# Slots, residual rows and final operations of the last products, and half of the divisions moved from ScalarE to VectorE

## The chip, the cores and the metric

The kernel runs on one core of a Trainium2 chip. The metric is the device time of one execution in microseconds, as the median of several runs. A profile of one execution gives the spans, waits and transfers that are read below. Its engines are TensorE (PE, and PEld for its weight loads), VectorE (DVE), ScalarE (ACT), GpSimd (POOL) and SyncE (SP, which issues most DMAs).

## The reference, cut to what matters

One layer of an encoder, for 1024 prompt rows and 32 sample rows with a cache of 512. All values are float32.

```python
def mla_attend(q_nope, q_rope, qpos, k_nope, k_rope, v, kpos):      # branch A, 8 heads, 64-wide values
    s = (einsum(q_nope, k_nope) + einsum(q_rope, k_rope)) * MLA_SCALE
    mask = (kpos // CHUNK) <= (qpos // CHUNK)                        # CHUNK = 64
    p = softmax(where(mask, s, NEG))
    return einsum('bhqs,bshd->bqhd', p, v)
...
merged = sigmoid(g_a) * (o_a @ w_proj_a) + sigmoid(g_b) * (o_b @ w_proj_b)   # branch B: stick-breaking attention
x = x + gt1 * rms_norm(merged @ w_out, g_post_mix)
h2 = rms_norm(x, g_pre_ffn) * (1 + sc2) + sh2
u = h2 @ w_up                                                        # 1024 -> 2 * 2816
y = causal depthwise conv of width 3 over u;  a, b = split(y)
f = (gelu(a) * b) @ w_down                                           # 2816 -> 1024
x = x + gt2 * rms_norm(f, g_post_ffn)
```

## The kernel before

A float32 product is made as three products of rounded parts: `hi` (line 61, ScalarE) writes the high half of a tile, `lo` (line 64, VectorE) the rest, and TensorE adds up high by high, high by low and low by high. The stages follow each other: modulation and projections, the stick-breaking attention, latents, the latent attention (about 675 to 945 us of the profile), merge, up-projection with convolution, down-projection (the end, from about 1560 us).

**The order on each engine** is not the program's. The framework plans it when the kernel is built: it plays the program through with costs of its own, gives each engine its next ready instruction, those earlier in the program first, and puts in the waits. The order on an engine and on a DMA queue is then fixed. Tiles come from pools; a tag has a set number of buffers, and a new tile waits until the oldest one of its tag is released.

**The latent attention** works head by head on pairs of query tiles of 128 rows (`attend`): tile `i` has `(i + 1) * 128` keys. For each tile, scores go to one or two PSUM banks, and `mla_weights` (from line 493 on) takes the maximum on VectorE (line 499), the exponential with its sum on ScalarE (line 507), the reciprocal `ri` of the sum on VectorE (line 514), and multiplies the whole tile by `ri` on ScalarE (line 515). Then the tiles are transposed (line 542), split (`PTh`, `PTl`) and multiplied by the values (line 555). Products of the other branch (`proj_b`) are planned in between. The second tile of each pair has 256, 512, 768 or 1024 keys.

**The down-projection** (`stage_down`) takes the gated rows `gdn` from DRAM and makes the product in a seven-product scheme on quarters (512 features by 512 rows), each in six steps over the 22 blocks of 128. Its matmuls are lines 1636 to 1638. `product(banks, s, weights, ...)` does one of the seven: at each step it takes weights that `put` has split into one of seven slots, loads the gates (`wr`, two buffers, line 1629), splits them (`wh`, `wl`, two buffers each) and issues 4 x 3 matmuls for each block of 128. `raw` loads weights into three `dr` buffers, and every fourth time into `wr` (a tile of its own, named `d` in the profile). Without a number, `put` takes the slots 0 to 6 in turn. Slots 0 to 3 are called `B` in the profile, 4 and 5 `d`, slot 6 `wh` and `wl`.

The last three products are that of `t3` with index 1 into the banks `X`, that of index 6 into the banks `Z`, whose loop also puts the six `t2` tiles into slots for later (`last`), and the last one, which is written out by hand: for each of four row tiles `t`, gates in blocks of 8 and 3 (line 1741), and 33 matmuls into `X[t]`. Between the first two, `c22[t]` is completed on VectorE (line 1714) and squared on ScalarE (line 1690).

`out` finishes a row tile of 128 rows: it loads the residual row `x1d` (line 1724), squares the half that has just come (`ps`), adds the sum of the other half (`s0`, line 1727, GpSimd), takes the root with `rstd` (lines 92 and 93, GpSimd), multiplies both halves by root and gain `G` (line 1732, VectorE), adds the residual (line 1733) and stores (line 1734). Its `x` and `y` come from tag `u` with five buffers, one of which holds `G`.

Of the kernel before, what the change touches and what calls it, by code (L numbers as in the profile page):

```python
# [8 lines left out]
F32 = mybir.dt.float32  # L9
# [8 lines left out]
P = 128  # L18
# [22 lines left out]
class K:  # L41
# [451 lines left out]
    def mla_weights(self, pieces, w):  # L493
        nc = self.nc
        B = self.tl(self.At, [P, TP], F32, "A")
        np_ = len(pieces)
        mx = self.tl(self.sm, [P, 2], F32, "mx")
        for i, (ps, c0, n) in enumerate(pieces):
            nc.vector.tensor_reduce(mx[:, i : i + 1], ps[:, :n], AX.X, ALU.max, negate=True)
        m = mx[:, 0:1]  # L500
        if np_ == 2:
            mn = self.tl(self.sm, [P, 1], F32, "mn")
            nc.vector.tensor_tensor(mn, mx[:, 0:1], mx[:, 1:2], ALU.min)
            m = mn
        sm = self.tl(self.sm, [P, 2], F32, "sum")
        for i, (ps, c0, n) in enumerate(pieces):
            self.exp = nc.scalar.activation(B[:, c0 : c0 + n], ps[:, :n], AF.Exp, bias=m, accum_out=sm[:, i : i + 1])
        s = sm[:, 0:1]
        rc = self.tl(self.sm, [P, 1], F32, "rc")
        if np_ == 2:  # L510
            nc.vector.tensor_tensor(rc, sm[:, 0:1], sm[:, 1:2], ALU.add)
            s = rc
        ri = self.tl(self.sm, [P, 1], F32, "ri")
        nc.vector.reciprocal(ri, s)
        nc.scalar.activation(B[:, :w], B[:, :w], AF.Identity, scale=ri)
        return B

    def attend(self, h, score, weights, V, out, order=(0, 1, 2, 3)):
# [1063 lines left out]
    def stage_down(self):  # L1582
# [29 lines left out]
        def raw(j, n, e, h):  # L1612
            self.n_raw += 1
            x = self.dn() if self.n_raw < 3 or self.n_raw % 4 else wr
            return load(x.rearrange("p (k c) -> p k c", k=2), j, n, e, h)

        def put(x, i=None):
            n = x.shape[1]
            if i is None:
                i = self.n_slot % len(slots)  # L1620
                self.n_slot += 1
            h, l = (y[:, :n] for y in slots[i])
            self.hi(h, x)
            self.lo(l, x, h)
            return h, l
# [14 lines left out]
        def product(banks, s, weights, first, more=None, part=range(6)):  # L1640
            for i, (j, n) in enumerate(steps):
                if i not in part:
                    continue
                wh, wl = weights(i, j, n)
                gh, gl = gates(s, j, n)
                if more:
                    more(i, j, n)
                for k in range(n):
                    for t in range(4):
                        tk = slice(t * P, t * P + P)  # L1650
                        add3(banks[t], gh[:, k, tk], gl[:, k, tk], wh[:, k], wl[:, k], first and j + k == 0, j + k == NJ - 1)
# [37 lines left out]
        def square(t, x, c):  # L1689
            nc.scalar.activation(junk, x, AF.Square, accum_out=c)  # L1690
# [22 lines left out]
        for t in range(4):  # L1713
            add(c22[t], X[t], c22[t], ALU.add)
            square(t, c22[t], ss[:, 4 + t : 5 + t])

        last = []
        product(Z, 6, lambda i, j, n: put(raw(j, n, 1, 1), (0, 1, 2, 3, 0, 1)[i]), False,
                lambda i, j, n: last.append(put(t2[i], (4, 5, 6, 2, 3, 0)[i])))

        def out(t, done, ps, s0, c0):

            x = tok()
            nc.sync.dma_start(x, self.x1d[t])
            s = self.tl(self.sm, [P, 1], F32, "ss")
            square(t, ps, s)
            nc.gpsimd.tensor_tensor(s, s, s0, ALU.add)  # L1727
            r = self.rstd(s, D, P)
            y = tok()
            for c, f in ((c0, ps), (512 - c0, done)):  # L1730
                c = slice(c, c + 512)
                nc.vector.scalar_tensor_tensor(y[:, c], f, r, G[:, c], ALU.mult, ALU.mult)  # L1732
                nc.vector.tensor_tensor(y[:, c], y[:, c], x[:, c], ALU.add)  # L1733
                nc.sync.dma_start(a["y_p"][0, t * P : t * P + P, c], y[:, c])

        for t in range(4):
            add(c12[t], Z[t], c12[t], ALU.add)
        for t in range(4):
            for k0, n in ((0, 8), (8, 3)):
                x = self.tl(self.W, [P, 1024], F32, "wr")  # L1740
                nc.sync.dma_start(x[:, : n * P].rearrange("p (k c) -> p k c", k=n),
                                  self.gdn[k0 : k0 + n, :, 1536 + t * P : 1536 + t * P + P].rearrange("k p c -> p k c"))
                gh, gl = (y.rearrange("p (k c) -> p k c", c=P) for y in self.wsplit(x, n * P))
                for k in range(n):
                    wh, wl = (y[:, (k0 + k) % 2] for y in last[(k0 + k) // 2])
                    add3(X[t], gh[:, k], gl[:, k], wh, wl, False, k0 + k == NJ - 1)
            out(t, c11[t], c12[t], ss[:, t : t + 1], 512)
            out(4 + t, c22[t], X[t], ss[:, 4 + t : 5 + t], 0)
        G2.release()
        self.F.release()  # L1750
        self.Rp.release()
# [89 lines left out]
```

## Time and profile before

| | |
|---|---|
| median of three runs | 1797.5 us (1796.99 to 1802.86) |
| the profiled execution | 1796.74 us, its span 1794.7 us |
| TensorE, VectorE, ScalarE, GpSimd busy | 97%, 70%, 56%, 14% of the span |
| granted clock of TensorE | 0.994 in the mean |
| HBM traffic | 174.32 MB read, 51.25 MB written |

A row in the order of time has its start, its length, engine, line, operation, what is written `<-` what is read, shapes, and in brackets the idle time of the engine before it with what ended it. A row of a group has count, then busy time in us and the mean of one in ns, then idle time before. A row of waits has the total, the number and the longest.

### The profile page before, as it was taken

What the parts mean: (1) busy time and instruction counts of PE and PEld (TensorE: products, weight loads), DVE (VectorE), ACT (ScalarE), POOL (GpSimd) and SP (SyncE); (2) the same over time, 40 slices, a digit from 0 to 9 for tenths busy, and PEclk for the clock granted to TensorE, in tenths of its full rate; (3) what the DMA queues carried; (4) which work ended last, traced back from release to release, by engine and by line L of the source; (5) the groups of instructions that cost most, each with busy time, mean ns of one, the idle gap of its engine ahead of it and who ended that gap; (6) DMA issues with size and microseconds to landing.
All of it is one profiled execution on the core that took longest, in us unless ns stands there. A gap on an engine that the chain in (4) does not pass through costs nothing. (4 is left out here: it accounts for less than half of the span.)

```text
span 1794.7 us, 30062 instructions
## 1 busy us (share of the span) xinstructions
PE 1733.5 (97%) x11610; PEld 1547.7 (86%) x11610; DVE 1258.4 (70%) x2087; ACT 1005.4 (56%) x1926; POOL 253.3 (14%) x518
## 2 busy tenths in 40 slices
PE   6999999999999999999999999999999999999997
PEld 3988888988888998888888868999999999977876
DVE  4677377576487467777676768977777787788446
ACT  4565366564464469688687357644444454544332
POOL 2112111110111001101000022321111111110001
PEclk9999999999999999999999999999999999999999
DMA  8333332332333112313336542333333323597426
GB/s 316 109 101 106 101 100 74 90 111 83 101 103 85 57 54 77 90 51 95 101 115 218 169 154 83 124 124 124 101 124 126 132 90 124 196 344 260 147 87 224
DMA packets 181710, 227.52 MB, mean 127 GB/s; under 512 B 13349, under 2 KB 129776, under 8 KB 181568
## 3 DMA queue, kind: packets, MB, share of 16 engines
q1 hardware_dynamic: 166048, 182.10, 31.7%
q0 software_dynamic: 15296, 43.42, 6.8%
q8 instruction: 91, 1.49, 0.3%
q14 instruction: 51, 0.42, 0.1%
q10 hardware_dynamic: 224, 0.09, 0.0%
HBM read 174.32 MB, written 51.25 MB: 126 GB/s over the span
## 5 line engine op out<-in xcount | busy, mean ns | idle before, releaser
L61 ACT ACTIVATE wh<-wr 128x1024 fp32r<-128x1024 f32 (+6 forms) x185 | 149.5, 818 | 254.9 <-PE s L1305 83.4
L64 DVE TENSOR_TENSOR wl<-wr,wh 128x1024 fp32r<-128x1024 f32 (+6 forms) x185 | 168.3, 916 | 137.0 <-ACT wh L61 135.5
L68 PE MATMUL mm<-hh,wh 128*128 128x352 f32 x696 | 229.6, 330 | 2.4 <-DVE nat L648 2.4
L69 PE MATMUL mm<-hl,wh 128*128 128x352 f32 x696 | 228.6, 328 | 0.4 <-DVE hl L277 0.4
L70 PE MATMUL mm<-hh,wl 128*128 128x352 f32 x696 | 228.0, 328 | 0.0
L68 PEld LDWEIGHTS mm<-hh,wh 128*128 128x128 f32 x696 | 131.3, 189 | 10.3 <-issue 4.1
L69 PEld LDWEIGHTS mm<-hl,wh 128*128 128x128 f32 x696 | 131.5, 189 | 2.7 <-DVE hl L277 0.9
L70 PEld LDWEIGHTS mm<-hh,wl 128*128 128x128 f32 x696 | 131.6, 189 | 1.2 <-issue 0.4
L542 PE MATMUL tr<-c,A 128*128 128x128 f32 x576 | 93.7, 277 | 4.9 <-ACT A L490 3.6
L1306 PE MATMUL s<-T,wl 128*128 128x256 f32 (+1 forms) x328 | 93.4, 285 | 0.0
L1305 PE MATMUL s<-T,wh 128*128 128x256 f32 (+1 forms) x328 | 93.3, 285 | 0.0
L1304 PE MATMUL s<-T,wh 128*128 128x256 f32 (+1 forms) x328 | 93.3, 284 | 0.0
L486 DVE TENSOR_TENSOR_SCAN A<-A 128x128 f32<-128x128 f32 (+8 forms) x66 | 87.8, 1343 | 0.4
L1442 DVE SCALAR_TENSOR_TENSOR u<-u,c,u 128x1058 f32<-128x1058 f32 x68 | 87.0, 1316 | 1.4 <-ACT u L1439 0.2
L490 ACT ACTIVATE A<-A 128x128 f32<-128x128 f32 (+8 forms) x66 | 44.6, 682 | 74.8 <-DVE A L489 74.3
L64 DVE TENSOR_TENSOR PTl<-tr,PTh 128x512 fp32r<-128x512 f32 x96 | 62.9, 683 | 29.9 <-ACT PTh L61 29.5
L542 PEld LDWEIGHTS tr<-c,A 128*128 128x128 f32 x576 | 67.5, 141 | 14.4 <-ACT A L490 8.1
L1304 PE MATMUL tr<-T,wh 128*128 128x272 f32 (+1 forms) x272 | 77.7, 286 | 0.0
L1306 PE MATMUL tr<-T,wl 128*128 128x272 f32 (+1 forms) x272 | 77.4, 285 | 0.0
L1305 PE MATMUL tr<-T,wh 128*128 128x272 f32 (+1 forms) x272 | 77.3, 284 | 0.0
L64 DVE TENSOR_TENSOR wl<-S,wh 128x1024 fp32r<-128x1024 f32 x40 | 48.9, 1223 | 37.8 <-ACT wh L61 37.8
L1304 PE MATMUL mm<-T,wh 128*128 128x256 f32 (+1 forms) x256 | 73.1, 286 | 0.0
(650 smaller groups left out, 5557.1 us busy)
## 6 DMA issues: line engine op xcount, KB each, us to landing
wr<-in_w_ada_dram SPq DMA_DIRECT2D x48, 512.0 KB, 4.7
wr<-in_w_up_dram SPq DMA_DIRECT2D x44, 512.0 KB, 3.8
dr<-in_w_down_dram SPq DMA_DIRECT2D x43, 512.0 KB, 5.8
wr<-gdn SPq DMA_DIRECT2D x34, 512.0 KB, 3.9
wr<-in_w_in_dram SPq DMA_DIRECT2D x33, 512.0 KB, 4.2
gdn<-u POOLq DMA_DIRECT2D x23, 512.0 KB, 4.8
gd<-nat POOLq DMA_DIRECT2D x48, 176.0 KB, 2.1
t<-gd SPq DMA_DIRECT2D x16, 528.0 KB, 5.2
```

Source lines behind the costliest of these rows:

```text
L61: self.nc.scalar.activation(out, in_, AF.Identity, scale=scale)
L64: return self.nc.vector.tensor_tensor(out, full, hi.bitcast(F32), ALU.subtract)
L68: m(ps, lh, rh, start=start, stop=False)
L69: m(ps, lh, rl, start=False, stop=False)
L70: m(ps, ll, rh, start=False, stop=stop)
L486: nc.vector.tensor_tensor_scan(r, r, r, 0.0, ALU.add, ALU.bypass)
L490: nc.scalar.activation(A[:, :w], A[:, :w], AF.Exp)
L542: nc.tensor.transpose(tr[:, (2 * s + q) * P : (2 * s + q + 1) * P], at[q][:, b * P : b * P + P], self.idt)
L1304: m(ps[:, :n], w[0][:, k], x[0][:, k, c], start=first and k == 0, stop=False, skip_group_check=True)
L1305: m(ps[:, :n], w[0][:, k], x[1][:, k, c], start=False, stop=False, skip_group_check=True)
L1306: m(ps[:, :n], w[1][:, k], x[0][:, k, c], start=False, stop=k == 3, skip_group_check=True)
L1442: nc.vector.scalar_tensor_tensor(y, u[:, w : w + YW], self.cvT[:, w, cc : cc + 1], y, ALU.mult, ALU.add)
```

## The change

The diff, whole but for blank lines:

```diff
@@ mla_weights
         nc.vector.reciprocal(ri, s)
-        nc.scalar.activation(B[:, :w], B[:, :w], AF.Identity, scale=ri)
+        if w % 256 == 0:
+            nc.vector.tensor_scalar(B[:, :w], B[:, :w], ri, None, ALU.mult)
+        else:
+            nc.scalar.activation(B[:, :w], B[:, :w], AF.Identity, scale=ri)
         return B
@@ stage_down
         for t in range(4):
             add(c22[t], X[t], c22[t], ALU.add)
             square(t, c22[t], ss[:, 4 + t : 5 + t])
+        nc.gpsimd.tensor_scalar(ss[:, :8], ss[:, :8], 1.0 / D, EPS, ALU.mult, ALU.add)
         last = []
-        product(Z, 6, lambda i, j, n: put(raw(j, n, 1, 1), (0, 1, 2, 3, 0, 1)[i]), False,
-                lambda i, j, n: last.append(put(t2[i], (4, 5, 6, 2, 3, 0)[i])))
-
-        def out(t, done, ps, s0, c0):
-
-            x = tok()
+        product(Z, 6, lambda i, j, n: put(raw(j, n, 1, 1), (2, 4, 6, 1, 2, 4)[i]), False,
+                lambda i, j, n: last.append(put(t2[i], (3, 5, 0, 6, 1, 2)[i])))
+
+        x1 = [x.rearrange("p k c -> p (k c)") for x in (*t3[:5], *t2[:3])]
+        for t, x in zip((0, 4, 1, 5, 2, 6, 3, 7), x1):
             nc.sync.dma_start(x, self.x1d[t])
-            s = self.tl(self.sm, [P, 1], F32, "ss")
+
+        def out(t, done, ps, c0):
+
+            x = x1.pop(0)
+            s, v, r = (self.tl(self.sm, [P, 1], F32, n) for n in ("ss", "rv", "rs"))
+            y = tok()
+            cd, cp = slice(512 - c0, 1024 - c0), slice(c0, c0 + 512)
+            nc.gpsimd.tensor_tensor(y[:, cd], done, G[:, cd], ALU.mult)
             square(t, ps, s)
-            nc.gpsimd.tensor_tensor(s, s, s0, ALU.add)
-            r = self.rstd(s, D, P)
-            y = tok()
-            for c, f in ((c0, ps), (512 - c0, done)):
-                c = slice(c, c + 512)
-                nc.vector.scalar_tensor_tensor(y[:, c], f, r, G[:, c], ALU.mult, ALU.mult)
-                nc.vector.tensor_tensor(y[:, c], y[:, c], x[:, c], ALU.add)
+            add(y[:, cp], ps, G[:, cp], ALU.mult)
+            nc.gpsimd.tensor_scalar(v, s, 1.0 / D, ss[:, t : t + 1], ALU.mult, ALU.add)
+            nc.gpsimd.tensor_tensor(r, v, self.mhalf, ALU.pow)
+            for c in (cp, cd):
+                nc.vector.scalar_tensor_tensor(y[:, c], y[:, c], r, x[:, c], ALU.mult, ALU.add)
                 nc.sync.dma_start(a["y_p"][0, t * P : t * P + P, c], y[:, c])
@@ the last product, written out
             for k0, n in ((0, 8), (8, 3)):
-                x = self.tl(self.W, [P, 1024], F32, "wr")
+                x = self.dn() if k0 == 0 else self.tl(self.W, [P, 1024], F32, "wr")
                 nc.sync.dma_start(x[:, : n * P].rearrange("p (k c) -> p k c", k=n),
...
-            out(t, c11[t], c12[t], ss[:, t : t + 1], 512)
-            out(4 + t, c22[t], X[t], ss[:, 4 + t : 5 + t], 0)
+            out(t, c11[t], c12[t], 512)
+            out(4 + t, c22[t], X[t], 0)
```

In words: the 32 second tiles of the pairs in the latent attention are multiplied by `ri` on VectorE instead of ScalarE. The last full product takes its weights and the `t2` tiles into other slots. The eight residual rows are loaded into tiles `t3` and `t2` that have been read, all asked for in the program ahead of the last product, and no longer into `u` buffers one by one. The sums of squares are scaled once for all eight, `out` multiplies the earlier half by `G` on GpSimd and the later one on VectorE, and then one operation on VectorE for each half multiplies by the root and adds the residual. The larger gate loads of the last product use the three `dr` buffers (`dn()`).

## Prediction

> **What bounds the kernel now.** I read the page first, then the windows over the places that the change touches, then the order of time there, and last the waits of TensorE.
>
> ```profile
> span 1794.7 us, 30062 instructions
> ...
> PE 1733.5 (97%) x11610; PEld 1547.7 (86%) x11610; DVE 1258.4 (70%) x2087; ACT 1005.4 (56%) x1926; POOL 253.3 (14%) x518
> ```
>
> TensorE is busy for 97% of the span. So work that the other engines gain or lose counts only where TensorE stands still, or behind its last matmul. The windows show where that is. Their columns are length, then busy time and instructions of TensorE, its weight loads, VectorE, ScalarE and GpSimd, then the granted clock, the share of the DMA engines, and GB/s.
>
> ```profile
> 675.00:945.00 270.00, 261.73 (x1761) 229.09 (x1760) 194.42 (x486) 220.06 (x521) 32.04 (x59) 0.99 0.29 88
> ...
> 1700.00:1716.00 16.00, 16.00 (x71) 12.86 (x70) 6.64 (x6) 4.80 (x7) 0.00 (x0) 1.00 0.27 82
> 1719.89:1721.70 1.81, 0.00 (x1) 0.00 (x1) 1.75 (x3) 1.81 (x5) 0.00 (x0) 1.00 0.84 269
> 1722.90:1726.40 3.50, 3.50 (x10) 2.68 (x10) 1.20 (x2) 0.17 (x2) 0.00 (x0) 0.51 0.50 140
> 1769.20:1769.79 0.59, 0.01 (x2) 0.01 (x1) 0.59 (x2) 0.50 (x3) 0.08 (x1) 1.00 0.80 316
> 1769.79:1777.70 7.91, 7.91 (x33) 6.11 (x33) 5.09 (x9) 2.03 (x4) 2.09 (x6) 1.00 0.92 318
> 1777.70:1779.44 1.74, 0.04 (x2) 0.00 (x1) 1.68 (x2) 1.10 (x4) 1.27 (x1) 1.00 0.64 234
> ```
>
> The first row is the latent attention: TensorE lacks 8.3 of 270 us there, ScalarE has 220 us of work (82%), VectorE 194 (72%). The rest is the end of the kernel. TensorE stands for 1.81 us between the product of `t3` and the product of `Z`, and 1.2 us after it has started again its clock is granted at 0.51 for 3.50 us, which costs 3.50 x 0.49 = 1.7 us. In the last product it stands for 0.58 and 1.70 us. Then comes the tail behind the last matmul.
>
> **Part 1, the slots of the last full product.** The seven slots are handed out in turn, and 30 puts come before the product of `Z` with index 6. The last six, of the product of `t3`, fill 3, 4, 5, 6, 0, 1, and slot 2 is free from its beginning. Before, the weights of the first two steps go to slots 0 and 1, which are the last two to come free.
>
> ```profile
> 1715.96 1.06 ACT L61 ACTIVATE wh<-wr 128x1024 fp32r<-128x1024 f32 x1 [4.02 <-PE tr L1637]
> 1716.89 0.69 DVE L1714 TENSOR_TENSOR d<-mm,d 128x512 f32<-128x512 f32 x1 [3.69 <-PE mm L1638]
> 1716.93 1.04 ACT L61 ACTIVATE B<-dr 128x1024 fp32r<-128x1024 f32 x1
> 1717.50 1.22 DVE L64 TENSOR_TENSOR wl<-wr,wh 128x1024 fp32r<-128x1024 f32 x1
> ...
> 1720.43 1.22 DVE L64 TENSOR_TENSOR B<-dr,B 128x1024 fp32r<-128x1024 f32 x1
> ...
> 1721.70 0.50 PE L1637 MATMUL s<-B,wh 128*128 128x512 f32 x1 [1.81 <-DVE B L64]
> ```
>
> The high half of slot 0 (`B<-dr`) is made at 1716.93, as soon as step 4 of `t3` has released it, and its low half comes behind the four additions to `c22` on VectorE, at 1720.43 to 1721.65. TensorE has done its four matmuls that need only high halves by 1719.89 and waits for it. After the change these weights go to slot 2, those of step 1 to slot 4 and those of step 2 to slot 6, the first `t2` tiles to 3, 5 and 0. All but the last of these are free while `t3` still runs; ScalarE has 4.80 and VectorE 6.64 us of work in the 16 us before, so both halves are made there. What is late next is the split of the gates, `wl<-wr,wh`, which ends at 1718.72, over a microsecond before TensorE stops at 1719.89. The stall of 1.81 us goes. The slow stretch goes with it, since no other stall lies in the 3.4 us ahead of it: 3.5 us together. Bounds: nothing is gained if another low half is put in the same place; were `wl` planned behind all four additions (0.6 us from start to start), it would end at about 1720.5, and some 1.1 us of the stall would stay. I take 3.5, because the row has `wl` behind one addition only. The puts that now wait for this product's own steps (slots 6, 1, 2 of `t2` tiles 3 to 5, and weights 4 and 5) are like three that wait there before; they are first read in the last product, or four steps later, so they cost nothing.
>
> [...]
>
> **Part 2, residual rows and loads of the last product.**
>
> ```profile
> 1768.51 1.69 DVE L64 TENSOR_TENSOR wl<-wr,wh 128x1024 fp32r<-128x1024 f32 x2
> ...
> 1769.76 0.38 SPq L1741 DMA_DIRECT2D wr<-gdn  x1
> ...
> 1775.71 1.06 ACT L61 ACTIVATE wh<-wr 128x1024 fp32r<-128x1024 f32 x1 [5.26 <-DMA wr<-gdn]
> 1776.95 1.29 DVE L1733 TENSOR_TENSOR u<-u,u 128x512 f32<-128x512 f32 x2 [1.83 <-DMA u<-x1d]
> ...
> 1778.16 1.27 POOL L1727 TENSOR_TENSOR ss<-ss,d 128x1 f32<-128x1 f32 x1 [5.94 <-ACT q L1690]
> 1778.17 1.22 DVE L64 TENSOR_TENSOR wl<-wr,wh 128x1024 fp32r<-128x1024 f32 x1
> ```
>
> The 1.70 us are explained here. The gates of the last quarter were asked for at 1769.76 on a DMA that is 92% busy, landed at 1775.7, and their low half stood behind two additions on VectorE that themselves waited 1.83 us for a residual row. The 0.58 us are the same queue: `wl` started only at 1768.51 behind the earlier final operations. The change takes both causes away. The eight `x1d` loads move off the `u` buffers and into `t3` and `t2` tiles that are read out during the products before, so seven of them leave the busy stretch and pass to one with a DMA share of 0.27. The gates of four quarters get three `dr` buffers beside the two `wr`, which are free once the product's weights lie in their slots, save one that is reloaded after the first quarter. On SP's queue the `x1d` loads wait for `t3` and `t2` and stand ahead of gates for the next products; two `wr` buffers mean that a gate load is issued over 8 us ahead of its use (a step is 24 matmuls of 0.24 us, as 33 take 7.91 us above: 5.7 us), so I cost this at nothing; without that cover the price would be a late load, like the 5.26 us that ScalarE waits here. The gain is 0.58 + 1.70 = 2.3 us at most. What is late next is the chain ScalarE high half, VectorE low half at each quarter's start: buffers come free nine matmuls (2.1 us) ahead, the two take 1.06 + 1.22 us, TensorE needs the low half two matmuls (0.5 us) in, so the slack is about 0.3 us less the handovers. A final operation that has just begun on VectorE (0.75 us) costs up to 0.6 us at each of three places: 0 to 1.8. VectorE has less to do than before (part 3), so I take 0.5. The gain: 1.8 us.
>
> **Part 3, the final operations.** The order of time after the last matmul:
>
> ```profile
> 1787.05 0.60 ACT L1690 ACTIVATE q<-tr 128x512 f32<-128x512 f32 x1 [4.74 <-PE tr L1638]
> 1787.54 0.19 ACT L1690 ACTIVATION_READ_ACCUMULATOR q<-tr 128x1 f32 x1
> 1787.81 0.19 POOL L1727 TENSOR_TENSOR ss<-ss,d 128x1 f32<-128x1 f32 x1 [6.40 <-ACT q L1690]
> 1788.09 0.19 POOL L92 TENSOR_SCALAR rv<-ss 128x1 f32<-128x1 f32 x1
> 1788.36 0.55 POOL L93 TENSOR_TENSOR rs<-rv,c 128x1 f32<-128x1 f32 x1
> 1788.94 0.75 DVE L1732 SCALAR_TENSOR_TENSOR u<-tr,rs,u 128x512 f32<-128x512 f32 x1 [2.96 <-POOL rs L93]
> 1789.61 0.74 DVE L1732 SCALAR_TENSOR_TENSOR u<-q,rs,u 128x512 f32<-128x512 f32 x1
> 1790.27 1.28 DVE L1733 TENSOR_TENSOR u<-u,u 128x512 f32<-128x512 f32 x2
> ```
>
> Two small GpSimd operations become one, since `ss` is scaled beforehand: 0.28 us from start to start. Two multiplications and two additions become two operations that do both: the last ends 1.47 us after the first has begun, not 2.61. The product with `G` moves ahead: that of the PSUM half takes 0.69 us on VectorE from 1787.1 or, should it have to follow the square, from 1787.7, and ends before the root (1788.64) either way. The end comes 2.61 - 1.42 + 0.28 = 1.5 us sooner. The other seven times, VectorE has three operations (2.1 us) for four (2.8), off the path. The new GpSimd products, `done` times `G`, have no like row: the nearest are
>
> ```profile
> L1432 POOL COPY c<-u 128x2 f32<-128x2 f32 x44 | 26.2, 595 | 251.8 <-DVE u L1378 227.4 <-ACT u L1517 24.4
> ...
> L424 POOL COPY ksb<-big 128x32 f32<-128x32 f32 x4 | 3.7, 926 | 82.7 <-ACT big L416 82.7
> ```
>
> so 11 ns a column, 6.2 us for 512 at the far end; VectorE's own 0.69 us is the near end. I take 1.5 us, nearer to VectorE's row because it is the one of that width. Eight of these, 12 us (at worst 50), lie in GpSimd's idle time: the inputs are ready once `c22` is added up (1720.4), and the last waits only for a `u` buffer that is free some 6 us ahead. The new operation on `ss` waits for the eighth square, which ScalarE makes at the boundary, and nothing behind it on GpSimd is needed before the last product.
>
> GpSimd can be held up: its 128x1 addition took 1.27 us at 1778.16 while VectorE ran a subtraction with two SBUF inputs, against 0.19 at 1787.81. [...]
>
> **Part 4, the division in the latent attention.**
>
> ```profile
> L515 ACT ACTIVATE A<-A,ri 128x1024 f32<-128x1024 f32 x8 | 9.2, 1155 | 0.3 <-DVE ri L514 0.2
> ...
> L515 ACT ACTIVATE A<-A,ri 128x768 f32<-128x768 f32 x8 | 7.5, 935 | 0.4 <-DVE ri L514 0.2
> ...
> L515 ACT ACTIVATE A<-A,ri 128x512 f32<-128x512 f32 x8 | 5.8, 722 | 0.0
> ...
> L515 ACT ACTIVATE A<-A,ri 128x256 f32<-128x256 f32 x8 | 4.1, 507 | 0.8 <-DVE ri L514 0.8
> ```
> ```profile
> L330 DVE TENSOR_SCALAR x<-x,rs 128x1024 f32<-128x1024 f32 x8 | 5.9, 751 | 4.4 <-POOL rs L93 4.2
> ...
> L353 DVE TENSOR_SCALAR xs<-xs,rs 128x256 f32<-128x256 f32 x1 | 0.4, 353 | 0.9 <-POOL rs L93 0.9
> ```
> ```profile
> PE pv L555 <- ACT PTh L61: 1.2, 1, 1.2
> PE pv L555 <- DVE PTl L64: 1.0, 4, 0.3
> ...
> PE tr L542 <- ACT A L515: 0.9, 2, 0.6
> ```
>
> The 32 tiles whose width is a multiple of 256 (eight heads, four each) leave ScalarE: 9.2 + 7.5 + 5.8 + 4.1 = 26.6 us. On a line between the two VectorE rows they take 0.35, 0.49, 0.62 and 0.75 us, 17.7 us in all. ScalarE falls from 220 to 193 us and VectorE rises from 194 to 212, 79% of the stage; behind each new operation stand reductions and low halves on VectorE's queue, up to 0.75 us later. The operation itself waits only for the reciprocal just before it. The weights are ready 0.15 to 0.4 us sooner. The gain is bounded by what TensorE waits for ScalarE (1.2 + 0.9 in these rows; with smaller ones about 3) and one slow stretch of 1.7 us: 4.8. The loss is bounded by all 17.7 us, were VectorE the limit throughout. I take 0.9 us of gain, the wait for `L515` itself, since TensorE's waits for the two engines are alike and both stay under 80%.
>
> **The sum.** 3.5 + 1.8 + 1.5 + 0.9 = 7.7 us. The profiled execution took 1796.7 us (span 1794.7); less 7.7 that is 1789.0. The median of the runs shown is 1797.5, 0.8 above it, so I forecast a median of 1789.8.
>
> **The rivals.** Within 0.3% (5.4 us: 1792.1 to 1802.9) is what a measurement of this kernel can hardly tell from no change.
>
> The boundary's stall only changes its name: low halves of the gates or of another put stand behind the additions, and half of part 1 and all of the left-over 1.8 us of part 2 are lost: 1789.8 + 1.8 + 1.3 = 1792.9. For it speaks that VectorE has 1.75 us of work in the 1.81 us of the stall; against it that three of its operations move ahead. Chance 0.15. The change then does only part of what it says.
>
> The slow stretch stays, because something else than the stall brings it: 1789.8 + 1.7 = 1791.5. Against it: it begins 1.2 us after the stall, and the 1.70 us gap later has none. Chance 0.08. [...]
>
> GpSimd's long products hold VectorE: four of them meet low halves that TensorE waits for, 0.7 to 1.5 us each, about 4 us: 1793.8. For it the 1.27 us row, against it that there it is GpSimd that waits. Chance 0.12.
>
> Slower: VectorE becomes the limit of the latent attention. From 17.7 us added, more than 13.1 must reach TensorE (7.7 - 0.9 of gains elsewhere, and 5.4 past the bound): 1803 to 1808. Against it 72% now. Chance 0.05.
>
> ScalarE was the limit there: 4.8 us for 0.9, 1785.9. Chance 0.12.
>
> **How the numbers follow.** The likeliest case has 0.48, of which 0.45 lies below 1792.1; with it go the ScalarE case (0.12), most of the slow stretch (0.06), and a fifth of the first and third rivals (0.05): faster 0.68. Slower has the VectorE case and 0.01 beside it, 0.06; same the rest, 0.26. The range, 1785.0 to 1796.5, takes in the gain's bound of part 4 with no stall left in part 2, and above it the two partial cases together.
>
> **What would show it.** TensorE without a gap between 1715 and 1728 and at a clock of 1.00; the first `B` low halves of `Z` ahead of that boundary; `x1d` loads issued before 1730; no `wr<-gdn` wait on ScalarE in the last product, and gaps there below 0.6 us; about 1.4 us from the root to the last VectorE operation; L515 left with 34 operations on ScalarE. Wrong it would be with a new wait for `wl` or `PTl` on TensorE above 2 us, another slow stretch, or a GpSimd product of many us ahead of the last root.

## The result, and the profile after

The changed kernel takes 1788.2 us (median of six runs, 1786.87 to 1790.57), the kernel before 1797.8 us beside it: a ratio of 0.9942, 95% interval 0.9928 to 0.9955. The forecast was 1789.8 us. The profiled execution took 1786.87 us, 9.9 us less than that of before, where the sum gave 7.7. Its page:

```profile
span 1784.7 us, 30053 instructions
...
PE 1731.1 (97%) x11610; PEld 1544.9 (87%) x11610; DVE 1270.6 (71%) x2111; ACT 982.6 (55%) x1894; POOL 270.8 (15%) x519
```

TensorE is the bound as before. The windows of the latent attention and of the boundary behind the product of `t3` (columns as in the prediction):

```profile
675.00:945.00 270.00, 263.41 (x1789) 230.55 (x1788) 211.90 (x524) 200.62 (x494) 32.86 (x59) 1.00 0.28 88
...
1716.00:1722.00 6.00, 6.00 (x27) 4.87 (x26) 6.00 (x6) 4.41 (x9) 5.13 (x4) 1.00 0.60 170
1722.00:1728.00 6.00, 6.00 (x27) 4.82 (x27) 3.50 (x5) 2.79 (x4) 0.00 (x0) 1.00 0.95 282
```

TensorE runs through the boundary without a gap and at full clock. The other signs that the prediction named are there too: the first low half of the `Z` weights (`B<-dr`) is made at 1687.24 us, the `x1d` loads are issued between 1662.3 and 1721.2 us, 34 divisions are left on ScalarE, ScalarE waits for no gates in the last product, and TensorE's longest gap there is 0.50 us. The end, in order of time:

```profile
1777.65 0.40 PE L1642 MATMUL tr<-B,wl 128*128 128x512 f32 x1
1778.16 0.60 ACT L1694 ACTIVATE q<-tr 128x512 f32<-128x512 f32 x1 [6.07 <-PE tr L1642]
1778.66 0.19 ACT L1694 ACTIVATION_READ_ACCUMULATOR q<-tr 128x1 f32 x1
1778.88 0.69 DVE L1739 TENSOR_TENSOR u<-tr,u 128x512 f32<-128x512 f32 x1 [3.35 <-ACT q L1694]
1778.95 0.27 POOL L1740 TENSOR_SCALAR rv<-ss,d 128x1 f32<-128x1 f32 x1 [5.00 <-ACT q L1694]
1779.30 0.55 POOL L1741 TENSOR_TENSOR rs<-rv,c 128x1 f32<-128x1 f32 x1
1779.88 1.42 DVE L1743 SCALAR_TENSOR_TENSOR u<-u,rs,d 128x512 f32<-128x512 f32 x2 [0.31 <-POOL rs L1741]
```

From the start of the last square to the end of VectorE it was 4.50 us (1787.05 to 1791.55), and is 3.14 (1778.16 to 1781.30).

Where the 9.9 us between the spans come from, by the starts of matmuls in the two traces (the second stretch ends at the last value product that reads `PTl`):

| stretch | before | after | difference |
|---|---|---|---|
| to the first score of the latent attention | 670.91 | 671.84 | +0.9 |
| first score to last value product of `PTl` | 268.21 | 263.09 | -5.1 |
| to the first matmul of the down-projection | 623.57 | 624.50 | +0.9 |
| first to last matmul of the down-projection | 223.84 | 218.22 | -5.6 |
| last matmul to the end of the span | 8.14 | 7.08 | -1.1 |

### The profile page after: what moved, and what is told of

Same layout as the page of the kernel before. It is cut to its first block, busy times and chain, and to the rows that moved or that the text cites. A ratio compares the mean times of both kernels' runs of the same rounds, so it can differ in the third digit from the quotient of the medians.

```text
span 1784.7 us, 30053 instructions
## 1 busy us (share of the span) xinstructions
PE 1731.1 (97%) x11610; PEld 1544.9 (87%) x11610; DVE 1270.6 (71%) x2111; ACT 982.6 (55%) x1894; POOL 270.8 (15%) x519
## 4 chain that ended last, share of the span: by engine, by line
PE 43%; DVE 3%; ACT 2%; issue 1%; DMA 1%; POOL 1%; DVEq 0%; POOLq 0%; ACTq 0%; SPq 0%
PE s L1310 3%; PE s L1308 3%; PE s L1309 3%; PE tr L1308 2%; PE tr L1310 2%; PE tr L1309 2%; PE mm L1308 2%; PE mm L1310 2%; PE mm L1309 2%; PE tr L1642 1%; PE tr L1641 1%; PE tr L1640 1%; PE s L70 1%; PE s L68 1%; PE s L1642 1%
## 5 line engine op out<-in xcount | busy, mean ns | idle before, releaser
L61 ACT ACTIVATE wh<-wr 128x1024 fp32r<-128x1024 f32 (+6 forms) x181 | 145.7, 812 | 240.9 <-PE s L1309 82.0
L64 DVE TENSOR_TENSOR wl<-wr,wh 128x1024 fp32r<-128x1024 f32 (+6 forms) x181 | 164.4, 916 | 126.9 <-ACT wh L61 125.8
```

The costliest lines, as they stand in the source:

```text
L61: self.nc.scalar.activation(out, in_, AF.Identity, scale=scale)
L64: return self.nc.vector.tensor_tensor(out, full, hi.bitcast(F32), ALU.subtract)
```

## The experiments

Medians are beside runs of before on the same chip (1797.2 to 1797.8 us). Matmul lengths are those of the table's second and fourth stretch. A slow stretch is one in which the profile has TensorE's clock at half for one interval of 3.41 us, unless more is said.

| kernel | median us | ratio (95%) | attention | down-projection |
|---|---|---|---|---|
| before | | | 268.2, 2 slow stretches | 223.8, 1 slow |
| after | 1788.2 | 0.9942 (0.9928 to 0.9955) | 263.1 | 218.2 |
| e_after | 1788.5 | 0.9947 (0.9933 to 0.9961) | 263.4 | 218.9 |
| e_mla | 1794.8 | 0.9981 (0.9971 to 0.9992) | 263.3 | 222.1 |
| e_slots | 1794.7 | 0.9984 (0.9975 to 0.9994) | 268.7, 2 slow | 221.1 |
| e_tail | 1792.3 | 0.9968 (0.9955 to 0.9980) | 266.2 | 218.7 |
| e_noslots | 1791.8 | 0.9968 (0.9958 to 0.9979) | 263.1 | 222.6, 1 slow |
| e_p2 | 1788.3 | 0.9947 (0.9934 to 0.9961) | 263.0 | 219.4 |
| e_vec | 1786.2 | 0.9936 (0.9922 to 0.9950) | 263.5 | 218.3 |
| e_early | 1788.2 | 0.9941 (0.9927 to 0.9956) | 263.1 | 218.2 |
| e_odd | 1792.4 | 0.9967 (0.9956 to 0.9979) | 265.2 | 218.8 |
| e_all | 1793.1 | 0.9972 (0.9961 to 0.9983) | 269.4, 1 slow | 219.6 |
| e_order | 1791.5 (one run) | | 267.9, 2 slow (3.41 and 6.83 us) | 217.3 |

### The division alone, and the rest alone

`e_mla` is before with the new branch in `mla_weights`. `e_tail` is after without it.

```diff
# e_tail
-        if w % 256 == 0:
-            nc.vector.tensor_scalar(B[:, :w], B[:, :w], ri, None, ALU.mult)
-        else:
-            nc.scalar.activation(B[:, :w], B[:, :w], AF.Identity, scale=ri)
+        nc.scalar.activation(B[:, :w], B[:, :w], AF.Identity, scale=ri)
```

> The kernel before with the new division alone; the rest, the end included, is as before. The profiles of before and after differ by 5.1 us between the first scores of the latent attention and the end of it, where 0.9 us was forecast; 3.4 us of that are two stretches of 3.41 us at half the clock (at 869.62 and 913.99 us of before) that after does not have. Theory A (the division takes away waits for ScalarE, and with them the slow stretches): 4 to 5 us faster than before, no half-clock stretch between 675 and 945 us, TensorE busy for about 263.4 of 270 us there. Theory B (the slow stretches are an accident of one execution and the waits alone count): 0.9 to 1.7 us faster. Theory C (VectorE now is the limit there and the stage loses): slower than before. The order that is planned for all engines changes with this edit, also outside of the stage: if the gain lies outside of 670 to 945 us, it is owed to the order and not to the division.

> The changed kernel with all divisions back on ScalarE, so the change of the down-projection alone. Its profile after shows 5.5 us less from the first to the last matmul of that stage and 1.2 us less behind the last matmul. Theory A (the parts add up): 6.7 us faster than before, the latent attention with its half-clock stretches as before. Theory B (the division's order of work also helped the last stage): 4 to 5.5 us faster.

Measured: `e_mla` 2.9 us faster than before (by the interval 1.4 to 5.2), `e_tail` 5.4 (3.6 to 8.1): 8.3 together, where the whole change gave 9.6 and, in the runs of `e_after`, 8.7. The median of `e_mla` is between theories A and B. The traces say why. With the divisions on ScalarE the attention took 268.2 us in before and 266.2 in `e_tail`, whose order there is the same, but which had no slow stretch. So the two slow stretches of before made 2.0 of its 5.1 us, and 3.1 are owed to the new kernel. The slow stretches are not all chance, though: of three profiles with the old order of this stage (before, `e_slots`, `e_tail`) two have them, of the eight with the order of after none. Theory C falls. The median of `e_tail` lies in theory B (4 to 5.5 us), but its interval takes in the 6.7 of theory A as well; the traces have 5.1 us less in the down-projection and 1.1 us less behind it.

### The slots alone, and all but the slots

```diff
# e_slots: before with these lists; e_noslots: after with the old ones
-put(raw(j, n, 1, 1), (0, 1, 2, 3, 0, 1)[i])  ...  put(t2[i], (4, 5, 6, 2, 3, 0)[i])
+put(raw(j, n, 1, 1), (2, 4, 6, 1, 2, 4)[i])  ...  put(t2[i], (3, 5, 0, 6, 1, 2)[i])
```

> The kernel before with the new slot numbers of the product with index 6 alone. Theory A (the stall of 1.81 us brings the slow stretch of 3.41 us behind it): both go, 3.5 us faster than before. Theory B (the stretch has another cause): 1.8 us faster, a half-clock stretch left near 1722 us. Theory C (another low half takes the place of the one that was late): under 1.2 us, with a new wait of TensorE for a low half between 1715 and 1730 us.

> The changed kernel with the old slot numbers of the product with index 6. The new numbers alone took 3.0 us off the median of before. Theory A (the parts add up): 3 us slower than the changed kernel, 6.6 faster than before, with a stall of about 1.8 us near 1720 us. Theory B (the slow stretch at half the clock follows such a stall only where the stall lies within one interval of a grid of 3.413 us, on which all slow stretches of the traces begin and end, so that its phase decides in each execution): 1.8 us slower in executions without, 3.5 in those with it, and if the profile shows the stretch, more than half of one interval is idle ahead of it. Theory C (the new order of residual rows and final operations takes the stall away as well): no slower.

Measured: `e_slots` is 2.9 us faster than before by the ratio (1.1 to 4.5), `e_noslots` is 6.0 us faster than before by the medians, where after was 9.6 and 8.7: the slots are worth 2.7 to 3.6 us there. In `e_slots` the stall and the slow stretch behind it are gone, and no new wait lies between 1715 and 1730 us, so its theory C falls; the interval holds both 3.5 (A) and 1.8 us (B). Its down-projection is only 1.0 us shorter than that of `e_mla`, which has no slow stretch there either: the other waits of that stage are 3.4 us in all, where `e_mla` has 2.4. Of this difference 0.6 us lie at 1632.84 us, far ahead of the new slots, and 0.4 in the last product. In the full change nothing takes that back: `e_noslots`, less 1.7 us for its slow stretch, is at 220.9, after at 218.2 and 218.9.

The profiles with the old slots (before, `e_mla`, `e_noslots`) all have the stall, but only two of them a slow stretch behind it. Here are the windows of `e_mla` and the row that ends its stall, then those of `e_noslots` and of before. They are cut at the clock's own transitions, or a whole number of 3.413 us from one:

```profile
1718.75:1722.16 3.41, 2.06 (x9) 1.71 (x10) 3.41 (x4) 2.41 (x7) 0.00 (x0) 1.00 0.36 133
1722.16:1725.57 3.41, 3.41 (x17) 2.73 (x16) 0.16 (x1) 0.74 (x1) 0.00 (x0) 1.00 0.71 229
```
```profile
1720.10 0.50 PE L1641 MATMUL s<-B,wh 128*128 128x512 f32 x1 [1.82 <-DVE B L64]
```
```profile
1717.38:1720.79 3.41, 1.05 (x5) 0.86 (x5) 3.41 (x4) 2.91 (x8) 3.41 (x3) 1.00 0.50 152
1720.79:1724.21 3.42, 3.42 (x9) 2.67 (x8) 2.28 (x2) 0.00 (x0) 1.11 (x2) 0.50 0.77 227
```
```profile
1719.54:1722.95 3.41, 1.60 (x7) 1.05 (x6) 3.32 (x5) 3.38 (x8) 0.00 (x0) 1.00 0.52 156
1722.95:1726.36 3.41, 3.41 (x9) 2.64 (x8) 1.15 (x2) 0.12 (x2) 0.00 (x0) 0.50 0.51 140
```

The stall is the same in `e_mla` (1.82 us) and in before (1.81). In before it lies within one interval, of which TensorE works 1.60 us, and the next interval is at 0.50. In `e_mla` it is spread over two; the one that holds most of it still has 2.06 us of work, and the clock stays. In `e_noslots` the stall is 2.36 us long, all in one interval. Theory B holds, and theory C of `e_noslots` falls.

That stall is 0.54 us longer than in `e_mla`. The low half that TensorE waits for took 1.76 us for 1.22, since one of the new GpSimd products was running from 1717.37 to 1718.63 us (more on this below):

```profile
1717.95 1.76 DVE L64 TENSOR_TENSOR B<-dr,B 128x1024 fp32r<-128x1024 f32 x1
...
1719.77 0.50 PE L1641 MATMUL s<-B,wh 128*128 128x512 f32 x1 [2.36 <-DVE B L64]
```

So in the whole change the new slots also spare a delay that part 3 brings.

### What decides the clock

```diff
# e_grid: after, with slot 0 for all weights put in turn and one to three writes of their high halves
-            n = x.shape[1]
+            n, r = x.shape[1], 1
             if i is None:
-                i = self.n_slot % len(slots)
+                i, r = 0, 1 + self.n_slot % 3
                 self.n_slot += 1
             h, l = (y[:, :n] for y in slots[i])
-            self.hi(h, x)
+            for _ in range(r):
+                self.hi(h, x)
```

> A measurement of the clock, not a version: the changed kernel, but all weights that are put into slots in turn go into slot 0, and their high half is written once, twice or three times, in turn. So TensorE stalls before about 30 steps of the down-projection for some 1.5, 2.6 or 3.6 us. Before, e_slots and the others show 16 transitions of the clock, all within 0.01 us of a grid of 3.413 us of their own execution; the stall of 1.81 us brought a slow stretch in before (0.53 of an interval idle) and none in e_mla (the same stall over two intervals, 0.40 idle at most). Theory A (the share of an interval decides): each slow stretch begins at the end of an interval of that grid that was idle for more than about half, and none begins after others: after none of the 1.5 us stalls, after about three in four of the 2.6 us stalls and nearly all of the 3.6 us stalls. Theory B (the length of the gap decides): all gaps above one length bring a stretch, at a fixed time behind the gap and not on a grid.

It takes 1908.8 us (one run). Its trace has 38 transitions of the clock behind the first one at 25.89 us, and all of them lie within 0.013 us of multiples of 3.4133 us from it. Windows cut on that grid, in two parts, and the matmuls that end the stalls in them:

```profile
1671.13:1674.54 3.41, 1.74 (x8) 1.07 (x6) 3.41 (x5) 1.87 (x2) 1.28 (x1) 1.00 0.69 222
1674.54:1677.95 3.41, 3.16 (x12) 2.29 (x13) 3.28 (x4) 2.92 (x9) 0.00 (x0) 1.00 0.20 77
...
1681.36:1684.77 3.41, 0.91 (x4) 0.67 (x4) 2.15 (x2) 2.42 (x3) 0.00 (x0) 1.00 0.14 19
1684.77:1688.18 3.41, 3.41 (x9) 2.48 (x8) 0.30 (x1) 0.00 (x0) 0.00 (x0) 0.50 0.35 135
...
1691.59:1695.01 3.42, 0.00 (x0) 0.00 (x0) 1.23 (x1) 3.36 (x4) 0.00 (x0) 1.00 0.09 11
1695.01:1698.42 3.41, 2.92 (x6) 1.92 (x7) 1.23 (x1) 0.39 (x1) 0.00 (x0) 0.50 0.19 71
```
```profile
1674.73 0.73 PE L1641 MATMUL mm<-B,wh 128*128 128x512 f32 x2 [1.86 <-ACT B L61]
1683.87 0.73 PE L1641 MATMUL mm<-B,wh 128*128 128x512 f32 x2 [2.95 <-ACT B L61]
1695.46 1.22 PE L1641 MATMUL mm<-B,wh 128*128 128x512 f32 x2 [4.03 <-ACT B L61]
```

The slow stretch begins 0.90 us after the stall of 2.95 us and 0.45 us before the end of that of 4.03: at the tick, not at a fixed time behind a gap. Of the intervals at full clock from 1560 to 1850 us, 40 were idle for 0 to 0.485 and followed by full clock, 18 were idle for 0.61 to 1.00 and followed by half. Eight slow intervals that were idle for 0.09 to 0.26 were followed by another slow one, 18 without idle time by full clock. That is theory A, with other counts: all stalls from 2.26 us on were followed, where three in four of the middle length were expected. The six of 1.86 us were not. In this kernel alone a limit on the gap's length would part the stalls too; the pair of before and `e_mla` above excludes it.

Some intervals do not fit an idle share of one half by the records. One that was idle for 0.15 to 0.20 near 866 us was followed by a slow one in before, `e_slots`, `e_all` and `e_order`; its work is partly transposes and matmuls of 64 rows. In the same stage so were one near 911 us, idle for 0.46, in before and `e_slots`, and one at 882.45 us, idle for 0.24, in `e_order`, whose slow interval at 885.86 had no idle time and was still followed by another. And one of after at 1776.49, idle for 0.54 behind the last matmul, was not followed by a slow one. How the different matmuls count stays open.

### Late loads

```diff
# e_p2: after, part 2 undone
-            x = x1.pop(0)
+            x = tok()
+            nc.sync.dma_start(x, self.x1d[t])
...
-                x = self.dn() if k0 == 0 else self.tl(self.W, [P, 1024], F32, "wr")
+                x = self.tl(self.W, [P, 1024], F32, "wr")
```

> The changed kernel with part 2 undone: the residual rows are loaded into u buffers one by one in the final operations and all gates of the last product into the two wr buffers. The prediction gave part 2 1.8 us (the stalls of 0.58 and 1.70 us gone, 0.5 left). Theory A (late loads make those stalls): 1.5 to 2.5 us slower than the changed kernel, with ScalarE waiting some 5 us for gates and TensorE 1 to 2 us for a low half near 1775 us. Theory B (the shorter final operations alone free VectorE in time): under 0.7 us slower.

Measured: 1788.3 against 1788.5 us for after beside it; the down-projection is 0.4 to 1.1 us longer than in the two traces of after, 0.4 of it in the last product. The rows that theory A needs are not there:

```profile
1754.36 0.50 PE L1642 MATMUL mm<-B,wl 128*128 128x512 f32 x1 [0.67 <-DVE wl L64]
...
1770.21 0.50 PE L1642 MATMUL tr<-B,wl 128*128 128x512 f32 x1 [0.26 <-DVE wl L64]
...
1772.63 0.53 ACT L61 ACTIVATE wh<-wr 128x384 fp32r<-128x384 f32 x1 [1.52 <-DMA wr<-gdn]
```

One load is late, by 1.52 us where it was 5.26, and TensorE does not wait for it. The gaps of the last product are 0.67 and 0.26 us, not 0.58 and 1.70. Theory B is right: the new final operations alone take most of these stalls away. What part 2 would take away without them was not run.

### GpSimd's products

```diff
# e_vec
-            nc.gpsimd.tensor_tensor(y[:, cd], done, G[:, cd], ALU.mult)
+            add(y[:, cd], done, G[:, cd], ALU.mult)
# e_early: that line goes, and y[:, cd] below becomes done
             square(t, c11[t], ss[:, t : t + 1])
+            add(c11[t], c11[t], G[:, :512], ALU.mult)
...   (behind the product with index 6)
+        for t in range(4):
+            add(c22[t], c22[t], G[:, 512:1024], ALU.mult)
```

> The changed kernel with the product of the finished half and G on VectorE, not on GpSimd. In the profile after, eight such products on GpSimd take 1.29 to 2.2 us each, and VectorE's operations beside them are stretched (a low half from 1.22 to 2.10 us at 1752.92, for which TensorE waits 0.50 us at 1755.08). Theory A (the two engines hold each other up, and VectorE has room): the low halves are back at 1.22 us, the stall of 0.50 us is gone, VectorE's products take 0.69 us each: 0.5 us faster than the changed kernel, about 10 us faster than before. Theory B (eight operations, 5.5 us, on VectorE's queue delay low halves as much): no difference from the changed kernel within 0.5 us, with other waits for low halves. Theory C: VectorE's queue is the limit of the last product: 1 us or more slower than the changed kernel.

> A version that may beat the changed kernel: the product of the finished half and G is made on VectorE in place and early (of c11 behind its squares, of c22 behind the loop of the product with index 6), so that neither GpSimd nor the last product has it. With the product on VectorE inside of the final operations the median was 1786.2. Theory A (GpSimd's products cost 0.5 to 1 us by holding VectorE's low halves up, and VectorE has idle time in the two products before): 0.5 to 1.5 us faster than the changed kernel, no low half above 1.3 us, TensorE's waits for low halves from 1562 us on under 0.8 us in all. Theory B (what is left of the waits is the order of the splits, not the products): the same as the changed kernel within 0.5 us.

In after, GpSimd's products and VectorE's low halves hold each other up. First GpSimd's rows, then VectorE's beside them, and the matmul that waits:

```profile
1714.39 2.21 POOL L1737 TENSOR_TENSOR u<-d,u 128x512 f32<-128x512 f32 x1 [91.08 <-DMA dr<-gdn]
...
1752.65 1.29 POOL L1737 TENSOR_TENSOR u<-d,u 128x512 f32<-128x512 f32 x1 [5.65 <-DMA out_dram<-u]
```
```profile
1714.23 1.22 DVE L64 TENSOR_TENSOR wl<-wr,wh 128x1024 fp32r<-128x1024 f32 x1
...
1718.86 2.31 DVE L64 TENSOR_TENSOR B<-d,B 128x1024 fp32r<-128x1024 f32 x1
...
1752.92 2.10 DVE L64 TENSOR_TENSOR wl<-dr,wh 128x1024 fp32r<-128x1024 f32 x1 [1.91 <-ACT wh L61]
...
1755.08 0.50 PE L1642 MATMUL mm<-B,wl 128*128 128x512 f32 x1 [0.50 <-DVE wl L64]
```

The rows show more than contention: the operation that starts second is the longer one, by about the time that the first still has to run. At 1714.23 VectorE is first and takes 1.22 us, GpSimd's product 2.21. At 1752.65 GpSimd is first and takes 1.29 us, VectorE's low half 2.10.

In `e_vec` the last two of these low halves are back at 1.22 us, and TensorE does not wait at that place:

```profile
1721.04 1.22 DVE L64 TENSOR_TENSOR B<-d,B 128x1024 fp32r<-128x1024 f32 x1
...
1755.68 1.22 DVE L64 TENSOR_TENSOR wl<-dr,wh 128x1024 fp32r<-128x1024 f32 x1 [1.91 <-ACT wh L61]
```

So the engines do hold each other up, as theory A has it. But the time in the traces hardly moves: the down-projection takes 218.3 us in `e_vec` and 218.2 in `e_early`, as in one trace of after and 0.6 below the other, since a wait of 0.8 to 0.9 us for a low half of the gates appears elsewhere in both. It lies at 1594.9 us, far ahead of the edited operations; after has no wait there, `e_after` one of 0.29. By the medians `e_vec` is 11.5 us faster than before and `e_early` 9.0, where after was 9.6 and 8.7. The intervals of the ratios overlap widely, and neither version is shown to beat the changed kernel. For `e_early` that is its theory B; for `e_vec` the runs do not part A from B, and C falls.

### Other placings of the division

```diff
# e_odd                              # e_all
-        if w % 256 == 0:            +        nc.vector.tensor_scalar(..., ri, None, ALU.mult)   for every w
+        if w % 256:
```
```diff
# e_order: e_tail, with a copy of the reciprocal
+        r2 = self.tl(self.sm, [P, 1], F32, "r2")
+        nc.vector.tensor_copy(r2, ri)
-        nc.scalar.activation(B[:, :w], B[:, :w], AF.Identity, scale=ri)
+        nc.scalar.activation(B[:, :w], B[:, :w], AF.Identity, scale=r2)
```

> The changed kernel with the other half of the divisions on VectorE: the first tile of each pair (widths 128, 384, 640, 896) and not the second. ScalarE loses 23 us and not 26.6. Theory A (it is the engine's time that counts): within 1 us of the changed kernel. Theory B (it is the latency of the second tile, for which the transposes wait): 1 to 3 us slower than the changed kernel, and TensorE again waits about 0.9 us for the division on ScalarE before a transpose. The order planned for all engines changes with it.

> The changed kernel with every division of the latent attention on VectorE (66 tiles and not 32). In after ScalarE has 203 and VectorE 213 us of work in 272 us of that stage; the 34 divisions left on ScalarE take 23 us there and would take some 16 on VectorE: 180 and 229 us. Theory A (what the division saves is ScalarE's time, and VectorE has room): 1 to 3 us faster than the changed kernel, so 10.5 to 12.5 faster than before. Theory B (VectorE becomes the limit, or its queue delays the low halves): 1 to 4 us slower than the changed kernel, with TensorE waiting for VectorE in that stage.

> The change of the down-projection with all divisions on ScalarE (e_tail), and a copy of each reciprocal (128 x 1) on VectorE before its use. It moves no division, but the planner makes another order of all engines from it, as it did for each other placing of the divisions. From the first scores to the end of the latent attention it took 269.0 us in e_tail without a slow stretch, 265.9 to 266.2 in four profiles with 32 divisions on VectorE, 267.8 with the other 34. Theory A (moving the divisions gives the 3 us): 269 to 271 us here, less 1.7 for each slow stretch. Theory B (the order as such moves the stage by some us, whatever the engine): anywhere from 265 to 272 us.

> The changed kernel as it is, once more, beside the versions of this call and for comparison with the medians of the others. 9.6 us faster than before (1788.2), between 8 and 11. By theory A (the share of an interval idle decides the clock) no slow stretch between 670 and 945 us and none near 1720 us; by the theory that these went by chance, one of them in some profile.

`e_odd` is 5.4 us faster than before by the medians, where after was 9.6 and 8.7; its attention is 1.8 to 2.1 us longer than in the two traces of after, and its profile has a slow stretch at 1036.27 us, between the stages, that theirs have not (`e_noslots` has one at 1031.30). In the attention that is the size of its theory B, by the medians it is more (3.3 to 4.2 us), and the wait that B names is 0.5 us and not 0.9. `e_all` is 4.7 us faster than before, so 4.0 to 4.9 slower than after: the direction of its theory B. But that VectorE has become the limit is not shown. The two longest of TensorE's waits in that stage are

```profile
PE mm L68 <- ACT nat L1076: 1.3, 2, 0.7
PE tr L542 <- DVE A L515: 0.8, 1, 0.8
```

and the first is for ScalarE. The attention takes 266.2, 263.1 and (with a slow stretch) 269.4 us for 0, 32 and 66 divisions on VectorE. `e_after` was as expected: no slow stretch in the attention or near 1720 us.

`e_order` is the surprise. It moves no division, and VectorE has a copy of 0.15 us more to do at each. First the windows of the attention in `e_tail`, `e_order` and after, from the first score to the last value product of `PTl`, then that of two of the slow intervals of `e_order`, then three of TensorE's waits in it (total, number, longest):

```profile
670.55:936.77 266.22, 257.43 (x1751) 224.59 (x1751) 194.92 (x486) 219.20 (x523) 32.14 (x59) 1.00 0.29 89
```
```profile
671.43:939.34 267.91, 260.71 (x1752) 228.02 (x1751) 200.68 (x552) 217.97 (x523) 32.02 (x59) 0.98 0.29 89
```
```profile
671.84:934.93 263.09, 256.50 (x1750) 223.65 (x1748) 207.62 (x518) 196.65 (x491) 32.86 (x59) 1.00 0.29 90
```
```profile
885.86:892.69 6.83, 6.83 (x28) 5.79 (x27) 3.41 (x13) 3.02 (x9) 0.57 (x1) 0.50 0.26 83
```
```profile
PE pv L557 <- DVE PTl L64: 1.8, 6, 0.6
...
PE tr L544 <- ACT A L517: 0.5, 1, 0.5
PE pv L557 <- ACT PTh L61: 0.5, 1, 0.5
```

It takes 267.9 us with 10.24 us at half the clock (868.80 to 872.21 and 885.86 to 892.69). At the granted clock of 0.50 slow stretches cost at most half their length, 5.1 us here; the two of before, by `e_tail`, cost 1.0 each, perhaps because TensorE would have waited for part of that time anyway: 3.0 for 10.24 us. Without them its attention would take an estimated 262.8 to 264.9 us, 1.3 to 3.4 below `e_tail`. Theory A expects at least 269 us, in a measure that ends 2.7 us later, at the last value product of all. By it `e_order` has 265.5 to 267.6 us without the slow stretches: theory B, as far as one run can tell. TensorE's idle time in the attention says the same: 8.8 us in `e_tail`, 7.2 in `e_order`, 6.6 in after. ScalarE has as much work as in `e_tail` (218 and 219 us). So another order alone can give a good part of the 3.1 us that the moved divisions seem to give, 1.3 us or more. The waits for `PTh` (1.2 us in before) and for the division (0.9) are 0.5 us each here. Which part of the 3.1 us is the division's own stays open: no kernel here moved it and kept the order.

## Why the prediction was right, and where not

**Part 1, 3.5 us.** Right in place and about right in size: 2.9 alone (1.1 to 4.5), 2.7 to 3.6 in the whole. The mechanism is half right. The stretch at half clock does follow from the stall, but not in each execution: it came where 0.53 (before) and 0.69 (`e_noslots`) of the interval ahead of it were idle, and not where the stall left at most 0.40 of one idle (`e_mla`). The 3.4 us ahead of the stretch in which the prediction looked for other stalls are, by the traces, one such interval of 3.413 us; in before it holds no idle time but the 1.81 us of the stall. Of three profiles with the stall two have it, of ten others without the stall none. So the 1.7 us are had only in a part of the executions. What the prediction said against its rival (the stretch begins 1.2 us after the stall, and the gap of 1.70 us has none) was a matter of 0.53 and 0.50 of an interval, not of the length, and so near to a half the records do not part the cases cleanly (0.54 once without a slow stretch, 0.46 twice with one). A stall of 1.81 us was followed by half the clock in before, and one of 1.82 us in `e_mla` was not.

**Part 2, 1.8 us.** This step failed. Undone, it costs nothing that the medians show and 0.4 to 1.1 us in the traces. The prediction read the last row before the stall, a late residual row ahead of `wl`, as the cause; the shorter final operations on VectorE take most of the stalls away without the new loads. So part 3, which had been given only the tail, is enough for most of the gain booked under part 2; whether part 2 would have been enough by itself is open. The sum of both is right: stalls of 0.58 and 1.70 us went, and one of 0.50 came, put at 0.5.

**Part 3, 1.5 us.** 1.36 measured in the last chain, term by term as forecast (1.42 us for the two last operations, one small operation of GpSimd less). The prediction has 1.47 us for these two in one sentence and 1.42 in its sum; the rows beside it give 1.41, so the sum stands. The product with `G` did follow the square, the later of the two starts considered, and ended before the root. GpSimd's products took 1.28 to 2.27 us for the 1.5 taken. That nothing would come of them was too simple: the row of 1.27 us, for 0.19, shows GpSimd held by VectorE, and the traces of after show VectorE held by GpSimd as well, where GpSimd's product starts first (a low half of 2.10 us at 1752.92, for 1.22). But of the 4 us of that rival only 0.5 reached TensorE in this trace.

**Part 4, 0.9 us.** The term that was mis-sized. VectorE's operations came at the interpolated durations:

```profile
L517 DVE TENSOR_SCALAR A<-A,ri 128x1024 f32<-128x1024 f32 x8 | 6.0, 749 | 0.1
...
L517 DVE TENSOR_SCALAR A<-A,ri 128x256 f32<-128x256 f32 x8 | 2.8, 353 | 0.4
```

The gain was 5.1 us in the two traces, near the bound of 4.8 that the rival on ScalarE had, and 2.9 in the median. 2.0 of it are the two slow stretches of before, which `e_tail` shows that not every execution has. The other 3.1 are not just the wait for `L515`: 2.2 are less idle time of TensorE, by the windows of `e_tail` and after, and 0.9 less busy time; three weight loads fewer lie in the stretch (1748 for 1751). The prediction held the order of all other work fixed, and the planner made a new one, in which TensorE waits less for `PTh` and `PTl` too (1.2 and 1.0 us before):

```profile
PE tr L546 <- DVE A L517: 0.8, 2, 0.4
...
PE pv L559 <- ACT PTh L61: 0.4, 1, 0.4
...
PE pv L559 <- DVE PTl L64: 0.2, 1, 0.2
```

The wait for the division itself, the 0.9 that was taken, has hardly changed (0.8): it is now one for VectorE. And `e_order` shows that an order alone can be worth a good part of what was gained.

**What held the time near the forecast.** For the down-projection and the tail the prediction has 3.5 + 1.8 + 1.5 = 6.8 us; the traces have 5.6 + 1.1 = 6.7, and the median of `e_tail` 5.4 (3.6 to 8.1). The whole came out as near as it did partly by luck: 5.1 us in the attention for 0.9, and 1.9 given back ahead of the attention and between the stages, where nothing was forecast. At the start after's execution has 13.65 us at half clock and before's 6.83; `e_after` has 10.24, so this part changes from one execution to the next. Why the 0.9 us between the stages were lost stays open.

## What to carry to other kernels

Before a gain is credited to an edit, ask what a planner makes of the rest: make an edit that moves no work and see how far the stage moves by the order alone. In these traces a stall of TensorE of 1.81 us or more was followed by 3.41 us or more at half clock in some cases and not in others: behind all 18 intervals of `e_grid` that were idle for 0.61 to 1.00, behind one idle for 0.53 in before, behind none of the six stalls of 1.86 us in `e_grid`. So count such a stall as itself plus a part of another 1.7 us (half of 3.41), and do not take a slow stretch in one trace for a property of the kernel before other traces of the same order have it too. Where a wait has two causes in a row, undo each by itself; the row named last need not be the one whose removal pays.

## What the runs showed of the hardware

All slow stretches of all traces begin on a grid of 3.4133 us, and all end on it but the last, which the end of the trace cuts: from the start of the first one, to within 0.004 us in before and after and to 0.013 in `e_grid`. The phase of the grid differs from one execution to the next: the first slow stretch begins at 26.53 us in before, at 25.45 in after and at 24.25 in `e_after`, the same kernel as after. Much of the scatter goes with the time at half clock: of 46 runs of before beside the experiments, the ten with a mean granted clock of 0.993 took 1800.6 us in the mean, the eleven with 0.996 took 1795.8.

A product of 128 x 512 on GpSimd with two SBUF inputs and a subtraction of 128 x 1024 on VectorE with two SBUF inputs held each other up in after: the product took 1.28 to 1.29 us where it started first and 2.13 to 2.27 where it started second; VectorE's subtraction took 1.22 and 1.23 us where it was first (1714.23, 1769.19) and 1.50 to 2.31 behind a product (1717.15, 1718.86, 1752.92, 1761.36). VectorE's additions with one input in PSUM were not held there: three beside the product at 1622.02 us took 0.68 us each, and the product 1.29.
